# A hybrid decoder step: the projections of the 32 sample tokens as four partial sums in the four 32-column strips of the array

## The chip, the cores and the metric

The kernel runs on one core of one Trainium2 chip. The metric is the device time of one execution in microseconds (us). The kernel before takes 2430.94 us, the median of three runs (2429.08 to 2435.89).

## The reference, cut to what matters

One inference step of a two-layer decoder with model width 1024, for a prompt of 2048 tokens and for 8 decode sequences of 4 tokens each, the 32 "sample" tokens. Both pass through the same weights:

```python
def even_mixer(h, w_in, ...):            # layer 0: HGRN2 heads beside forgetting-attention heads
    proj = h @ w_in                      # 1024 -> 4100 columns
    ...
    out = jnp.concatenate([o_a, o_b], axis=-1) @ w_out
def odd_mixer(h, w_in, ...):             # layer 1: GLA
    proj = h @ w_in                      # 1024 -> 3088 columns
    ...
    return o @ w_out, s
```

All is float32. Each layer starts with an RMSNorm, ends with a residual add, and a last RMSNorm follows layer 1. What the change touches is a few of the matrix products above, and of them the rows of the 32 sample tokens alone: (32 x 1024) times (1024 x 256, 260 or 272).

## The kernel before, in words

**Numbers.** A float32 matrix product is made of three float16 products: activations and weights are each split into a high and a low half (`act` and `W`, both of class `Parts`, L95: a pair of views of one tile), and `mm3` (L451) adds high x high, high x low and low x high in PSUM. The fourth, low x low, isn't needed. The sum over 1024 rows takes 8 steps of 128, so a full product is 24 matmuls.

**Tokens.** The prompt is worked off in two halves of 1024 tokens. The 32 sample tokens ride with the first half, as columns 1024 to 1055 of `act`.

**Units.** The weights come in units of 256 columns (one of 260, one of 272). `half_unit` (L301) returns steps that fetch, measure, scale and split a unit, and `staged` (L1040) runs these steps for later units between the pieces of the present unit's product. There are two kinds of product. `proj_fm` (L457) is feature-major: the weights stand in the array and the tokens stream. `proj_tm` (L466) is token-major: 128 tokens stand in the array, 256 weight columns stream, two token tiles share a PSUM tile, and a function `evac` takes the result out.

**The sample tile in `proj_tm`.** With the first half come nine token tiles, eight of 128 tokens and one of 32. For units of 256 columns the tile of 32 goes to `few_rows` (L485). It first copies the sample tokens, once for all units of a stage, into a small tile `sam` that holds high and low halves side by side (L492, VectorE). Then 8 matmuls, one for each 128 rows of the sum, have the 64 columns (32 high, 32 low) standing and 512 columns streaming, which are 256 high and 256 low weight columns (`W.both`):

```python
nc.tensor.matmul(ps[: 2 * TS], self.sam[:, k].rearrange("p a t -> p (a t)"), W.both[:, :, k, :256], ...)
```

This gives all four products in four places of one PSUM tile `pS`. ScalarE copies one of them out (L498), VectorE adds two others to it (L500, two instructions), and low x low is left behind. The two wide units, `Bv0` (260 columns) and `Cv0` (272), take the ordinary way: 24 matmuls of `mm3` with 32 columns standing, evacuated from PSUM straight away.

**Which units are token-major.** In the first half of layer 0's input projection: `Ai0`, `Ai1` (`mk_v`, L793; their tiles are named `Av`), `Bk0`, `Bk1`, `Bv1` and the wide `Bv0` (`mk_bkv`, L870). In layer 0's output projection for the first half: `o00` to `o03` (`out_units`, L1610). In layer 1's input projection for the first half: the wide `Cv0` and `Cv1`, `Cv2`, `Cv3` (`mk_v`, L1666). In layer 1's output projection for the first half: `o10` to `o13`. These are 16 units of 256 columns and the two wide ones. For `Cv0` the last 16 columns are `r`, the input of the gate, which VectorE scales (L1685 to L1687), TensorE transposes (L1689, `prT`) and VectorE stores (L1690).

**PSUM.** The results of projections use the tag `pj`, with 3 buffers; `gr` has 2, `st` 1 and `o` 2.

**What sets the order.** Python generators issue the instructions. `mux` (L73) interleaves two generators by the costs that they yield: linear attention of one head (`lin_attn`, L512) runs beside the units of the next heads. After `few_rows`, `proj_tm` yields a cost of 1400 to it; other tiles yield 24 x 110 for each token tile. A scheduler then orders each engine's instructions by its own estimate of times, and each engine runs its list strictly in that order. So an instruction that waits holds back all that stand behind it on its engine.

**Work beside the sample tiles.** Within `lin_attn`, `levels` (L579) makes small matmuls (`gl`, L598) in strips of the array, and `decode` (L635) works on the states of the 8 sequences: `oS` (L676), four matmuls in four strips of 32 columns, then for every pair of sequences `stS` (L683, TensorE), a decay on GpSimd (L685) and an add on VectorE (L687). `stS` has one PSUM buffer, so each has to wait for the add of the one before it. In the attention over the paged cache there are two more places with four matmuls in four strips: the scores (L1416) and the forget biases (L1445).

## Time and profile before

| | |
|---|---|
| time of the profiled execution | 2431.39 us |
| its span, first to last instruction | 2429.7 us |
| around the span | 1.7 us |
| TensorE (PE) busy | 2316.8 us, 95% |
| VectorE (DVE) busy | 1463.1 us, 60% |
| ScalarE (ACT) busy | 1139.3 us, 47% |
| GpSimd (POOL) busy | 759.6 us, 31% |
| mean granted TensorE clock | 0.985 |

Times in the profile are microseconds from the start of the span, durations of single instructions are nanoseconds where it says so. PE is TensorE's matmuls, PEld its weight loads, which overlap the matmuls. L495 is line 495 of the kernel. A tile's name leaves out the buffer numbers: `pS_o` is the PSUM tile of `few_rows` in the output projections, whichever unit it is. In a row of the timeline stand the start, the time from the first start to the last end, the engine, the line, the operation, `out<-in`, the shape, and how many instructions of one kind were merged. A shape such as 128\*32 128x256 is a matmul with 128 rows and 32 columns standing in the array and 256 columns streaming. The end of a matmul is modelled and takes in its way through the array, so the times from start to start are what is to be read. Brackets at the end of a row give the time for which the engine was idle before it, and what ended that.

### The profile page before, as it was taken

The numbers are of one execution on the slowest core, as the hardware profiler recorded it, in microseconds if no ns is written. First come the engines' busy times: TensorE is split into PE (matmuls) and PEld (weight loads), VectorE is DVE, ScalarE is ACT, GpSimd is POOL, SyncE is SP. The second block draws the span as 40 slices with busy tenths as digits, with TensorE's granted clock in tenths as the row PEclk, the third lists the DMA queues.
The fourth block names the chain that finished last, engine by engine and source line by source line (L and its number), as shares of the span: only waits on it lengthen the run. The fifth ranks groups of instructions, "written<-read, shape, count | busy, mean of one in ns | idle before, by whom it ended". The sixth has DMA issues, their size and how long they took to land. (4 is left out here: it accounts for less than half of the span.)

```text
span 2429.7 us, 54346 instructions
## 1 busy us (share of the span) xinstructions
PE 2316.8 (95%) x21116; PEld 1637.8 (67%) x21116; DVE 1463.1 (60%) x3339; ACT 1139.3 (47%) x2513; POOL 759.6 (31%) x840
## 2 busy tenths in 40 slices
PE   7999999999999989999998999999999999998998
PEld 5667668855655875655445786777778766666887
DVE  7666657446765638667767353665675555557564
ACT  6434343343433126566667354545543645545243
POOL 3233323012213215234454221432443222322233
PEclk9999999999999999999999999999999999999999
DMA  6222235435431276776864631222246312114454
GB/s 183 73 80 80 67 111 166 142 107 146 144 115 59 85 227 204 227 250 205 274 209 141 191 107 44 63 75 76 67 141 192 117 37 70 44 58 152 142 195 153
DMA packets 296996, 316.97 MB, mean 130 GB/s; under 512 B 39729, under 2 KB 241010, under 8 KB 296738
## 3 DMA queue, kind: packets, MB, share of 16 engines
q1 hardware_dynamic: 295234, 308.98, 40.3%
q0 software_dynamic: 1504, 4.52, 0.5%
q8 instruction: 166, 2.72, 0.5%
q14 instruction: 92, 0.75, 0.1%
HBM read 242.31 MB, written 71.11 MB: 129 GB/s over the span
## 5 line engine op out<-in xcount | busy, mean ns | idle before, releaser
L453 PE MATMUL pt_o<-w_o,act 128*128 128x256 f16 x1024 | 282.8, 276 | 6.0 <-ACT w_o L335 5.1
L454 PE MATMUL pt_o<-w_o,act 128*128 128x256 f16 x1024 | 282.6, 276 | 1.1 <-POOL w_o L336 1.1
L455 PE MATMUL pt_o<-w_o,act 128*128 128x256 f16 x1024 | 282.6, 276 | 0.0
L453 PEld LDWEIGHTS <-act 128*128 128x128 f16 (+1 forms) x2320 | 228.7, 99 | 45.1 <-issue 14.3
L454 PEld LDWEIGHTS <-act 128*128 128x128 f16 (+1 forms) x2320 | 228.3, 98 | 33.1 <-issue 2.7
L455 PEld LDWEIGHTS <-act 128*128 128x128 f16 (+1 forms) x2320 | 228.4, 98 | 32.9 <-issue 4.3
L455 PE MATMUL pt_Cv<-w_Cv,act 128*128 128x256 f16 (+1 forms) x520 | 142.4, 275 | 0.0
L453 PE MATMUL pt_Cv<-w_Cv,act 128*128 128x256 f16 (+1 forms) x520 | 142.2, 275 | 0.0
L454 PE MATMUL pt_Cv<-w_Cv,act 128*128 128x256 f16 (+1 forms) x520 | 142.0, 275 | 0.0
L632 POOL TENSOR_TENSOR kA<-kA,fA 128x512 f32<-128x512 f32 (+1 forms) x56 | 80.8, 1442 | 195.7 <-PE gl_A L598 109.3
L1206 ACT ACTIVATE L<-L,nm,kc 128x512 f32<-128x512 f32 (+3 forms) x160 | 118.2, 741 | 35.5 <-DVE nm L1204 24.6
L632 POOL TENSOR_TENSOR kC<-kC,fC 128x512 f32<-128x512 f32 (+1 forms) x56 | 85.2, 1522 | 157.0 <-PE gl_C L598 76.4
L1214 POOL TENSOR_SCALAR L<-L,nm 128x512 f32<-128x512 f32 (+3 forms) x160 | 98.0, 626 | 79.3 <-DVE nm L1210 37.0
L1241 ACT ACTIVATE th<-pt 128x512 f16<-128x512 f32 (+3 forms) x159 | 80.4, 528 | 67.2 <-PE pt L1234 66.3
L1242 DVE TENSOR_TENSOR tl<-pt,th 128x512 f16<-128x512 f32 (+3 forms) x159 | 94.5, 608 | 25.9 <-ACT th L1241 25.3
L1234 PE MATMUL pt<-ident,L 128*128 128x128 f32 x544 | 91.0, 280 | 5.9 <-POOL L L1214 3.4
L1358 PEld LDWEIGHTS pkt<-ident,pgcache_fox_k 128*128 128x128 f32 x512 | 58.5, 143 | 46.7 <-issue 25.6
L1234 PEld LDWEIGHTS pt<-ident,L 128*128 128x128 f32 x544 | 67.2, 144 | 32.3 <-DVE tl L1242 8.4
L1358 PE MATMUL pkt<-ident,pgcache_fox_k 128*128 128x128 f32 x512 | 76.4, 282 | 11.4 <-DMA pgcache_fox_k<-in_cache_fox_k 7.8
L631 DVE TENSOR_TENSOR qC<-qC,fC 128x512 f32<-128x512 f32 (+1 forms) x56 | 53.5, 956 | 31.1 <-PE gl_C L598 30.2
L453 PE MATMUL pt_Bv<-w_Bv,act 128*128 128x256 f16 (+2 forms) x264 | 72.2, 273 | 0.0
L455 PE MATMUL pt_Bv<-w_Bv,act 128*128 128x256 f16 (+2 forms) x264 | 72.2, 273 | 0.0
(1088 smaller groups left out, 6887.8 us busy)
## 6 DMA issues: line engine op xcount, KB each, us to landing
pgcache_fox_k<-in_cache_fox_k SPq DMA_DIRECT2D x128, 256.0 KB, 4.1
pgcache_fox_v<-in_cache_fox_v SPq DMA_DIRECT2D x128, 256.0 KB, 4.0
yr<-yT SPq DMA_DIRECT2D x16, 1024.0 KB, 5.9
nx<-in_x_prompt SPq DMA_DIRECT2D x16, 512.0 KB, 4.8
wr_Aqf<-in_w_in_even SPq DMA_DIRECT2D x64, 128.0 KB, 2.8
wr_o<-in_w_out_even SPq DMA_DIRECT2D x32, 256.0 KB, 4.0
wr_Cv<-in_w_in_odd SPq DMA_DIRECT2D x32, 256.0 KB, 3.6
wr_Cqk<-in_w_in_odd SPq DMA_DIRECT2D x64, 128.0 KB, 2.6
```

What stands on the lines that cost most here:

```text
L453: nc.tensor.matmul(ps, lh[0], rh[0], start=first, stop=False)
L454: nc.tensor.matmul(ps, lh[0], rh[1], start=False, stop=False)
L455: return nc.tensor.matmul(ps, lh[1], rh[0], start=False, stop=last)
L631: nc.vector.tensor_tensor(xv[:, :, 1], xv[:, :, 1], t0.to_broadcast([P, nb, w]), ALU.mult)
L632: nc.gpsimd.tensor_tensor(kv[:, :, 0], kv[:, :, 0], t1.to_broadcast([P, nb, w]), ALU.mult)
L1206: self.last_exp = nc.scalar.activation(lt[:, :w], lt[:, :w], AF.Exp, bias=nm[:, 0:1], scale=ib, accum_out=nm[:, 2 + j : 3 + j])
L1214: nc.gpsimd.tensor_scalar(lt[:, :w], lt[:, :w], nm[:, 1:2], 2.0**14, ALU.mult, ALU.mult)
L1234: nc.tensor.transpose(pt[:, w : w + P], rows[b][s // 4][0][:, (s % 4) * P : (s % 4 + 1) * P], self.ident)
L1241: nc.scalar.activation(th[:, a:w], pt[:, a:w], AF.Copy),
L1242: nc.vector.tensor_tensor(tl[:, a:w], pt[:, a:w], th[:, a:w], ALU.subtract)))
L1358: nc.tensor.transpose(pk[:, j * P : (j + 1) * P], pgs[j][:, h * P : (h + 1) * P], self.ident)
```

## The change

`few_rows` no longer lets all four products come out of one wide matmul. It makes the three that are needed as matmuls of their own, 24 in all, each with 32 columns standing and the unit's width streaming. The 8 steps of the sum over 1024 rows are dealt out to four strips of 32 array columns: strip j takes steps j and j + 4 of each product, 6 matmuls that add up in PSUM partitions 32j to 32j + 31. Matmuls for the four strips are issued in turn. Then ScalarE copies strip 0's sum out, and VectorE adds those of the strips 1, 2 and 3, three adds in place of two. The wide units go the same way now, so `proj_tm` no longer has a path for a tile of 32 tokens, and the cost that it yields after `few_rows` is 700 in place of 1400. `Parts` no longer keeps the undivided tile.

```diff
@@ class Parts
-        self = super().__new__(cls, (both[:, 0], both[:, 1]))
-        self.both = both
-        return self
+        return super().__new__(cls, (both[:, 0], both[:, 1]))
@@ proj_tm
-            if n < P and width == 256:
-                evac(self.few_rows(pps, act, W, grp[0][0], nm), g, 1, n)
-                yield 1400
+            if n < P:
+                evac(self.few_rows(pps, act, W, grp[0][0], nm, width), g, 1, n)
+                yield 700
                 continue
@@ few_rows
-        ps = pps.tile([P, 2, 256], F32, tag="pj", name=f"pS_{nm}")
-        for k in range(KT):
-            nc.tensor.matmul(ps[: 2 * TS], self.sam[:, k].rearrange("p a t -> p (a t)"), W.both[:, :, k, :256],
-                             start=k == 0, stop=k == KT - 1)
-        t = self.few.tile([P, 512], F32, tag="c2", name=f"few_{nm}")[:TS, :256].unsqueeze(1)
-        nc.scalar.activation(t[:, 0], ps[:TS, 0], AF.Copy)
-        for r, c in ((0, 1), (TS, 0)):
-            nc.vector.tensor_tensor(t[:, 0], t[:, 0], ps[r : r + TS, c], ALU.add)
+        ps = pps.tile([P, width], F32, tag="pj", name=f"pS_{nm}")
+        for r in range(0, KT, 4):
+            for p, (x, y) in enumerate(((0, 0), (0, 1), (1, 0))):
+                for j in range(4):
+                    nc.tensor.matmul(ps[j * TS : (j + 1) * TS], self.sam[:, r + j, x], W[y][:, r + j, :width],
+                                     start=r + p == 0, stop=r > 0 and p == 2, tile_position=(0, j * TS))
+        t = self.few.tile([P, 512], F32, tag="c2", name=f"few_{nm}")[:TS, :width].unsqueeze(1)
+        nc.scalar.activation(t[:, 0], ps[:TS], AF.Copy)
+        for j in range(1, 4):
+            nc.vector.tensor_tensor(t[:, 0], t[:, 0], ps[j * TS : (j + 1) * TS], ALU.add)
         return t
```

In the order of the changed program, the 24 matmuls of a tile mostly stand together. In ten of the 18 tiles something stands between them: a transposition or a few small matmuls (`gl`, `stS`, `BkT`, `nt`), or some dozen matmuls of the next product. In `Cv1`, `Cv2` and `Cv3` these are `gl` and one `stS` pair after the first 10 of the 24 matmuls; before, they stood behind the whole tile and two more matmuls.

More of the change, by code (lines that the diff above doesn't have):

```diff
@@ L483, in proj_tm, with few_rows @@
             yield 24 * len(grp) * 110
-    def few_rows(self, pps, act, W, c0, nm):
+    def few_rows(self, pps, act, W, c0, nm, width):
         nc = self.nc
```

## The prediction

> **What bounds the kernel now.** I read the page first, then busy time by stage, then the timeline at the sample tiles.

> ```profile
> span 2429.7 us, 54346 instructions
> PE 2316.8 (95%) x21116; PEld 1637.8 (67%) x21116; DVE 1463.1 (60%) x3339; ACT 1139.3 (47%) x2513; POOL 759.6 (31%) x840
> PEclk9999999999999999999999999999999999999999
> ```

> ```profile
> 0.00:888.00 888.00, 854.65 (x8202) 602.67 (x8203) 537.74 (x1203) 337.63 (x763) 224.49 (x221) 1.00 0.37 113
> 888.00:1323.00 435.00, 399.31 (x2788) 233.86 (x2786) 297.76 (x931) 271.89 (x616) 196.11 (x311) 0.97 0.68 221
> 1475.00:2225.00 750.00, 729.98 (x7071) 523.30 (x7068) 443.19 (x818) 380.47 (x796) 237.12 (x207) 1.00 0.28 88
> 2225.00:2421.00 196.00, 192.06 (x1922) 165.35 (x1922) 109.41 (x212) 70.97 (x182) 59.48 (x64) 0.97 0.48 161
> ```

> TensorE is the bound: the first column after the length is its busy time, 96% of layer 0's projections (0 to 888 us), 97% of layer 1's (1475 to 2225) and 98% of the last products; its clock is nearly full. All sample tiles lie outside the attention stage (888 to 1323), the loosest. So time taken off TensorE's queue comes off the end, unless TensorE then arrives earlier at something that isn't ready. I therefore work out what a tile costs now, what it will cost, and at which places another engine eats the difference.

> **What a tile costs now.** One of the 16 narrow tiles, with the full-array matmuls around it:

> ```profile
> 391.27 0.27 PE L454 MATMUL pt_Bk<-w_Bk,act 128*128 128x256 f16 x1
> 391.38 0.27 PE L455 MATMUL pt_Bk<-w_Bk,act 128*128 128x256 f16 x1
> 391.58 1.92 PE L495 MATMUL pS_Bk<-w_Bk,sam_Av 128*64 128x512 f16 x8
> 393.43 0.28 PE L453 MATMUL pt_Bv<-w_Bv,act 128*128 128x260 f16 x1
> ```

> ```profile
> L495 PE MATMUL pS_o<-w_o,sam_o x64: 379/379/635, 1357.2 to 2336.9; 128*64 128x512 f16 x64
> L495 PE MATMUL pS_Cv<-w_Cv,sam_Cv x24: 379/379/404, 1540.3 to 1722.6; 128*64 128x512 f16 x24
> L495 PE MATMUL pS_Av<-w_Ai,sam_Av x16: 379/379/404, 51.9 to 217.8; 128*64 128x512 f16 x16
> L495 PE MATMUL pS_Bk<-w_Bk,sam_Av x16: 378/379/404, 391.6 to 453.1; 128*64 128x512 f16 x16
> L495 PE MATMUL pS_Bv<-w_Bv,sam_Av x8: 379/379/403, 484.3 to 485.9; 128*64 128x512 f16 x8
> ```

> From the last full-array matmul (391.38) to the next one (393.43) pass 2.05 us. Between full-array matmuls the step is 0.11 us (391.27 to 391.38); going over to 64 standing columns it is 0.20 (391.38 to 391.58). 64 + 24 + 16 + 16 + 8 = 128 matmuls, by 8 a tile: 16 tiles. A wide tile:

> ```profile
> 426.27 0.27 PE L455 MATMUL pt_Bv<-w_Bv,act 128*128 128x260 f16 x1
> 426.47 0.28 PE L453 MATMUL pt_Bv<-w_Bv,act 128*32 128x260 f16 x1
> 429.03 0.27 PE L455 MATMUL pt_Bv<-w_Bv,act 128*32 128x260 f16 x1
> 429.24 0.28 PE L453 MATMUL pt_Bk<-w_Bk,act 128*128 128x256 f16 x1
> ```

> 24 matmuls one after another, (429.03 - 426.47) / 23 = 0.111 us each, with the same 0.20 to go over and 0.21 to come back: 2.97 us. This also shows that a load of 32 columns per matmul fits behind 260 streamed columns of float16, in one strip.

> **What it will cost.** No float16 matmuls stand side by side in this trace, but float32 ones do:

> ```profile
> 1116.86 1.06 PE L1416 MATMUL sc<-kts,qz 128*32 128x512 f32 x8
> 1117.74 1.06 PE L1445 MATMUL sc<-suf,sel 128*32 128x128 f32 x32
> 1118.73 0.39 PE L453 MATMUL s<-h_k,h_q 128*128 128x512 f16 x1
> L1445 PEld LDWEIGHTS sc<-suf,sel x32: 109/110/111, 1117.3 to 1118.4; 128*32 128x32 f32 x32
> 2323.93 0.60 PE L563 MATMUL py_C<-ident,on_C 128*128 128x128 f32 x4
> ```

> L1445 runs 32 records, eight waves over the four strips. One alone would stream for about 0.11 us: the four full-array records of the last row take (0.60 - 0.28) / 3 = 0.107 from start to start, with 0.28 us the length of one, about that of the fp16 rows above. In a line 32 would need 3.5 us. They need 0.99 (1117.74 to 1118.73) with the way back to the full array: seven waves of 0.11 and 0.22 after the last one's start. The loads, one for each record and 110 ns long, don't show. A float16 matmul of 256 columns streams as long as such a record (0.11 us, rows above), so I take a **wave of 0.11 us**. Six waves: 0.20 + 5 x 0.11 + 0.22 = 0.97 us against 2.05, a gain of 1.08. The wave is bounded from below by the stream of one matmul, 0.11, and from above by four in a line, 0.44. I take 1.05, since the row's first wave comes from strips already and mine comes from the full array.

> [...]

> **The places.** Four full-mode interruptions cost a second way out and in, about 0.2 us each: in the changed order such work stands within `Av0`, `Av1`, `Bk0` and `o00`, where before it stood outside or the modes were alike. In `o10` two switches go, as `gl`, itself in strips, now follows directly. Net -0.6 us.

> `Bv0` gains 2.97 - 0.97 = 2.0. `Cv0` was cut up by other work:

> ```profile
> 1463.89:1469.99 6.10, 6.10 (x40) 3.12 (x38) 1.53 (x8) 1.07 (x4) 0.00 (x0) 1.00 0.00 0
> 1465.42 0.23 DVE L1687 SCALAR_TENSOR_TENSOR rt<-pt_Cv,kc,rh 128x16 f32<-128x16 f32 x1
> 1466.15 0.31 PE L1689 MATMUL prT<-ident,rt 128*80 128x128 f32 x1
> ```

> Of the 6.1 us about 2.0 are 13 matmuls of the next product (0.15 each), so 4.1 are the tile, with its many switches, and small transpositions. Now it takes some 1.2 with one split. But in the new order the transposition of the last full tile's `r` stands before it, and its input comes only at 1465.65, 1.8 us after that tile's last matmul (1463.89); and the tile now needs VectorE's copies into `sam`. I take 0.5 us of gain, between 0 and 3.

> `Cv1`, `Cv2`, `Cv3` are where another engine is late:

> ```profile
> 1540.35 1.91 PE L495 MATMUL pS_Cv<-w_Cv,sam_Cv 128*64 128x512 f16 x8
> 1542.19 0.32 PE L453 MATMUL pf_C01q<-act,w_Cqk 128*128 128x352 f16 x1
> 1542.60 0.71 PE L598 MATMUL gl_C<-qC,kC 128*24 128x16 f32 x64
> 1544.34 0.50 PE L683 MATMUL stS_C<-hl_C,kpad_C 96*128 96x256 f32 x2 [1.04 <-DVE s_C L687]
> ```

> ```profile
> 1536.73 1.82 DVE L660 TENSOR_TENSOR kpad_C<-hl_C,rowmask 96x512 fp32r<-96x512 f32 x2
> ...
> 1542.30 1.27 DVE L704 TENSOR_TENSOR vp_C<-vC,vp_C 128x256 fp32r<-128x256 f32 x1
> 1543.60 0.69 DVE L687 TENSOR_TENSOR s_C<-s_C,stS_C 128x512 f32<-128x512 f32 x1
> ```

> `stS` waits for VectorE's add, and VectorE is busy without a gap from 1536.7 up to it, with nothing of the sample tile ahead. So `stS` stays at 1544.3 however fast the tile is. In the new order only 10 of the 24 matmuls stand before it. The other 14 (3.5 waves and the way in and out, some 0.7 us) come behind it, and so do the two matmuls of the next product that stood before it (0.3): TensorE is 1.0 us later after `stS` than now. The last waits of the same chain can give that back, as it doesn't move either:

> ```profile
> PE py_C00S L563 <- ACT scT L606: 1.1, 1, 1.1
> ```

> I take a loss of 0.5 us for each of the three, between a gain of 1.05 and a loss of 1.1.

> **The evacuation.**

> ```profile
> L500 DVE TENSOR_TENSOR few_o<-few_o,pS_o x16: 397/410/414, 1362.2 to 2342.7; 32x256 f32<-32x256 f32 x16
> PE pt_Av L453 <- ACT act L448: 1.2, 1, 1.2
> ```

> One more add of 0.41 us for each narrow tile and a copy with three adds for the wide ones: some 9 us of VectorE, of which 40% is free. It holds a `pj` buffer 0.4 us longer, while two others let TensorE run on for two products; I cost it at nothing, and without that cover it would be 0.41 x 16 = 6.6 us. `Bv1` comes just before the second half's normalization, where TensorE already waits 1.2 us for ScalarE: I take 0.5 off there, between 0 and 1.05.

> **The sum.** 13 narrow tiles x 1.05 = 13.65, `Bv0` 2.0, `Cv0` 0.5, `Cv1` to `Cv3` -1.5, splits -0.6, `Bv1` -0.5: 13.5 us. From the profiled execution's 2431.4 (0.45 over the median of the three runs) that gives **2418 us**. With every tile's gain kept it is 21 us, 2410; with all the bounds on the bad side, 6.6 us of evacuation among them, some 4 us are left, 2427.

> **The rivals.**
> *Half-speed waves.* The four float16 strips get their weights or their columns only half as fast as the float32 ones, a wave of 0.22 us. For it speaks that a float32 wave of 512 columns takes 0.44 us (1116.86 to 1117.74, two waves), twice the time per column, so the float32 rows never asked for four strips at one column per 0.42 ns; against it that a float32 column is twice as many bytes. A tile then takes 1.63 us: the gain is 0.4 x 13 = 5.2, `Bv0` 1.3, `Cv0` 0, `Cv1` to `Cv3` -0.9 each (3.5 waves longer by 0.11 behind `stS`), splits and `Bv1` -1.1: 2.7 us, **2429 us**. [...]
> *Strips in a line* (slower). If float16 strips do not overlap at all, 24 matmuls of 0.111 and 0.41 for the switches are 3.0 us, 1.0 more than now: 13 x 1.0, three times 1.7 at `Cv1` to `Cv3` (the 0.5 and 14 x 0.11 - 3.5 x 0.11 behind `stS`), and the 1.1 of splits and `Bv1`, a loss of 19 us: **2450 us**. The sum changes sign at a wave of about 0.25 us. L1445 speaks against it.
> *Given back by the order.* The scheduler moved instructions of VectorE and ScalarE in the attention stage too, where no line changed; TensorE idles there for 435 - 399 = 36 us, and a quarter more of that, 9 us, would leave **2427 us**.

> **How the numbers follow.** Forecast 0.78, half-speed waves 0.09, in a line 0.05, given back 0.08. The forecast's own range is 2410 to 2427; to hold the time 8 times in 10 with half the chance of the first rival, I go to 2429. About 0.3% (7.3 us) is what a measurement of this kernel can tell from no change. Of the forecast 0.72 lie below 2423.6 and 0.06 above it; with most of the two middle rivals "same" has 0.21. Slower: the line, and 0.02 of an order gone worse, 0.07.

> **What would show it.** In the changed profile a tile's 24 records (128*32 128x256) from its last full-array neighbour to the next: 1.0 us is the forecast, 1.6 the first rival, 3.0 the second. `stS` at `Cv1` to `Cv3` should wait 2 us or more for L687. VectorE's add should be 0.41 us, and TensorE's matmuls after a tile should not wait for a `pj` buffer. Wrong it would be if the wave is over 0.2 us, or if TensorE's idle time in the attention stage or in the last products grows by several us.

## The result and the profile after

The changed kernel takes 2426.8 us (median of 20 runs, 2421.08 to 2431.52), the kernel before 2431.13 (20 runs): a ratio of 0.9982, 95% interval 0.9975 to 0.9989. It is faster by 4.3 us, where 13.5 were forecast. The profiled execution has a span of 2422.9 us, 2424.6 with the 1.7 around it, 2 us below the median. In what follows `Av00` is the prediction's `Av0`, `Cv01` its `Cv1`, and so on: the first digit is the half.

Two lines from the head of the page after, then busy time by stage (the same stretches as before; columns: PE, PEld, DVE, ACT, POOL, granted clock, DMA):

```profile
span 2422.9 us, 54885 instructions
PE 2300.0 (95%) x21372; PEld 1631.5 (67%) x21372; DVE 1478.9 (61%) x3361; ACT 1140.2 (47%) x2515; POOL 749.4 (31%) x840
```

```profile
0.00:888.00 888.00, 851.22 (x8279) 600.62 (x8280) 541.13 (x1211) 337.75 (x764) 222.69 (x221) 0.99 0.37 113
888.00:1323.00 435.00, 396.88 (x2792) 232.96 (x2791) 301.83 (x936) 278.86 (x627) 203.16 (x316) 0.97 0.68 223
1475.00:2225.00 750.00, 723.83 (x7074) 519.73 (x7073) 448.64 (x828) 377.77 (x794) 237.33 (x208) 0.99 0.29 87
2225.00:2421.00 196.00, 186.57 (x1984) 163.08 (x1982) 112.77 (x214) 70.83 (x181) 55.38 (x65) 0.98 0.49 164
```

TensorE has 16.8 us less to do (2316.8 to 2300.0), but its span shrank by only 6.8: the work went, the time stayed as idle time. In the four rows TensorE's free time grew by 3.4, 2.4, 6.2 and 5.5 us (888 - 851.22 against 888 - 854.65, and so on; roughly, since the stages begin up to 7 us earlier now, so that the last row takes in more of the kernel's end). The clock column fell from 1.00 to 0.99 in both stages of projections, which looks like nothing; but the clock records of both traces have 1.00 and 0.50 alone, so a mean of 0.99 over 750 us means 15 us at half clock (2 x 0.01 x 750; the records have 15.9 in the third row).

The tile itself is what was forecast. A narrow one with its neighbours in the timeline after, and the third add:

```profile
453.65 0.27 PE L453 MATMUL pt_Bk<-w_Bk,act 128*128 128x256 f16 x1
453.86 0.84 PE L495 MATMUL pS_Bk<-w_Bk,sam_Av 128*32 128x256 f16 x24
454.62 0.49 PE L247 MATMUL spr_o<-ident,kc 128*128 128x128 f32 x2
```

```profile
L500 DVE TENSOR_TENSOR few_o<-few_o,pS_o x24: 411/416/423, 1356.3 to 2339.4; 32x256 f32<-32x256 f32 x24
L495 PEld LDWEIGHTS <-sam_o x192: 92/97/152, 1349.7 to 2328.9; 128*32 128x32 f16 x192
```

From neighbour to neighbour pass 0.97 us (453.65 to 454.62), to the hundredth the working of the prediction; the way in is 0.21 (453.65 to 453.86). The 24 loads of 97 ns, 2.3 us in a line, don't show; nor do those of one strip in the prediction's wide tile, at 0.111 us a matmul with a load each. So both rivals about waves are out, with their 1.63 and 3.0 us.

Where the time stayed is seen at `Cv01`, TensorE first, then VectorE, then the windows of the stretch:

```profile
1531.69 0.50 PE L495 MATMUL pS_Cv<-w_Cv,sam_Cv 128*32 128x256 f16 x10
1532.72 0.70 PE L598 MATMUL gl_C<-qC,kC 128*24 128x16 f32 x64 [0.53 <-DVE rst_C00S L384]
1535.69 0.50 PE L683 MATMUL stS_C<-hl_C,kpad_C 96*128 96x256 f32 x2 [2.26 <-DVE s_C L687]
1536.12 0.61 PE L495 MATMUL pS_Cv<-w_Cv,sam_Cv 128*32 128x256 f16 x14
...
1538.69 0.50 PE L452 MATMUL pf_C01q<-act,w_Cqk 128*128 128x352 f16 x1
1538.99 0.50 PE L453 MATMUL pf_C01q<-act,w_Cqk 128*128 128x352 f16 x1
...
1540.71 0.31 PE L452 MATMUL pf_C01q<-act,w_Cqk 128*128 128x352 f16 x1
1540.86 0.31 PE L453 MATMUL pf_C01q<-act,w_Cqk 128*128 128x352 f16 x1
```

```profile
1533.64 1.27 DVE L704 TENSOR_TENSOR vp_C<-vC,vp_C 128x256 fp32r<-128x256 f32 x1
1534.94 0.69 DVE L687 TENSOR_TENSOR s_C<-s_C,stS_C 128x512 f32<-128x512 f32 x1
```

```profile
1533.00:1535.00 2.00, 0.42 (x51) 0.33 (x35) 1.97 (x3) 0.00 (x0) 2.00 (x3) 1.00 0.04 8
1536.40:1538.00 1.60, 1.60 (x19) 0.77 (x8) 1.52 (x3) 1.23 (x3) 1.29 (x2) 0.58 0.47 164
1538.00:1539.80 1.80, 1.80 (x8) 0.88 (x6) 1.76 (x4) 1.41 (x3) 1.80 (x2) 0.50 0.08 27
1541.00:1544.00 3.00, 3.00 (x81) 2.08 (x79) 2.18 (x5) 1.71 (x5) 0.74 (x1) 1.00 0.24 50
```

`stS` waits 2.26 us for the add L687 in place of 1.04, as forecast ("2 us or more"). What was not forecast stands behind it: the same matmul of 352 columns comes every 0.30 us (1538.69 to 1538.99) and later every 0.15 (1540.71 to 1540.86), and the granted clock is 0.50 in between. Behind the idle stretch (1533.4 to 1535.7) TensorE's clock is at 0.50 for 3.4 us (1536.6 to 1540.0 in the clock's records), and at 0.30 us a matmul in place of 0.15 these 3.4 us do 1.7 us less work than at full clock. `Cv02` and `Cv03` look the same.

The first tile, `Av00`, before and after:

```profile
51.94 1.91 PE L495 MATMUL pS_Av<-w_Ai,sam_Av 128*64 128x512 f16 x8 [1.56 <-DVE sam_Av L492]
54.49 0.32 PE L453 MATMUL pf_Ag<-act,w_Ag 128*128 128x352 f16 x1 [0.22 <-ACT w_Ag L335]
55.73 0.32 PE L455 MATMUL pf_Ag<-act,w_Ag 128*128 128x352 f16 x1 [0.76 <-POOL w_Ag L336]
```

```profile
52.51 0.62 PE L495 MATMUL pS_Av<-w_Ai,sam_Av 128*32 128x256 f16 x16
54.66 0.32 PE L451 MATMUL pf_Ag<-act,w_Ag 128*128 128x352 f16 x1 [1.53 <-ACT w_Ag L333]
56.25 0.45 PE L451 MATMUL pf_Ag<-act,w_Ag 128*128 128x352 f16 x1 [1.11 <-DVE pow_Aqf L265]
```

```profile
55.00:56.00 1.00, 0.14 (x1) 0.00 (x0) 1.00 (x4) 0.36 (x1) 1.00 (x2) 0.63 0.02 4
56.00:62.00 6.00, 5.75 (x20) 2.89 (x20) 5.62 (x19) 2.06 (x7) 3.80 (x10) 0.50 0.41 117
```

The next unit's weights `w_Ag` are still being split by ScalarE. The old tile covered that; now TensorE waits for it, and then runs 6 us at half clock. And behind `Bk00` stands a wait that is 0.19 us in the profile of before:

```profile
400.08 0.49 PE L754 MATMUL o_A<-v,scT 128*128 128x128 f32 x2 [1.42 <-ACT scT L606]
```

### The profile page after: what moved, and what is told of

The parts are those of the page before. It is cut to its first block, busy times and chain, and to the rows that moved or that the text cites. A ratio compares the mean times of both kernels' runs of the same rounds, so it can differ in the third digit from the quotient of the medians.

```text
span 2422.9 us, 54885 instructions
## 1 busy us (share of the span) xinstructions
PE 2300.0 (95%) x21372; PEld 1631.5 (67%) x21372; DVE 1478.9 (61%) x3361; ACT 1140.2 (47%) x2515; POOL 749.4 (31%) x840
## 5 line engine op out<-in xcount | busy, mean ns | idle before, releaser
L453 PE MATMUL pt_o<-w_o,act 128*128 128x256 f16 x1024 | 282.8, 276 | 0.0
L451 PEld LDWEIGHTS <-act 128*128 128x128 f16 x2304 | 227.0, 99 | 44.4 <-issue 11.6
L452 PEld LDWEIGHTS <-act 128*128 128x128 f16 x2304 | 226.8, 98 | 34.9 <-issue 4.9
L453 PEld LDWEIGHTS <-act 128*128 128x128 f16 x2304 | 226.7, 98 | 33.0 <-issue 4.3
L451 PE MATMUL pt_Cv<-w_Cv,act 128*128 128x256 f16 (+1 forms) x512 | 140.1, 275 | 1.5 <-ACT act L446 0.9
L453 PE MATMUL pt_Cv<-w_Cv,act 128*128 128x256 f16 (+1 forms) x512 | 140.2, 275 | 0.0
L452 PE MATMUL pt_Cv<-w_Cv,act 128*128 128x256 f16 (+1 forms) x512 | 139.8, 275 | 0.0
L1241 ACT ACTIVATE th<-pt 128x512 f16<-128x512 f32 (+3 forms) x159 | 81.2, 528 | 71.6 <-PE pt L1234 70.5
L451 PE MATMUL pt_Av<-w_Ai,act 128*128 128x256 f16 x256 | 70.5, 276 | 1.9 <-ACT act L446 1.9
L452 PE MATMUL pt_Av<-w_Ai,act 128*128 128x256 f16 x256 | 70.4, 275 | 0.8 <-POOL w_Ai L334 0.8
```

What stands on the lines that cost most here:

```text
L451: nc.tensor.matmul(ps, lh[0], rh[0], start=first, stop=False)
L452: nc.tensor.matmul(ps, lh[0], rh[1], start=False, stop=False)
L453: return nc.tensor.matmul(ps, lh[1], rh[0], start=False, stop=last)
L1241: nc.scalar.activation(th[:, a:w], pt[:, a:w], AF.Copy),
```

## The experiments

The theory tested: the strips bring about 1 us each, but at `Av00` and `Cv01` to `Cv03` a shorter tile only makes TensorE wait longer for another engine, and a wait of this length costs half the clock behind it. Rivals: the forecast's own terms for these places without the clock (A); the gain is lost elsewhere, through the new order or the evacuation (B).

All runs in one table. The last column is the time at half clock, mean over all runs of the kernel: 2 x (1 - granted clock) x span.

| run | tiles in strips | ratio to before, 95% | us at half clock |
|---|---|---|---|
| before | none | 1 | 68.0 |
| changed kernel | 18 | 0.9982 (0.9975 to 0.9989) | 81.5 |
| e1_but_cv | 15 | 0.9970 (0.9959 to 0.9982) | 77.9 |
| e2_but_av_cv | 14 | 0.9951 (0.9935 to 0.9968) | 70.2 |
| e12, the same again | 14 | 0.9958 (0.9941 to 0.9974) | 68.3 |
| e3_only_av_cv | 4 | 0.9990 (0.9978 to 1.0001) | 72.9 |
| e7_cv123 | 3 | 1.0030 (1.0017 to 1.0043) | 73.1 |
| e5_late8 | 8 | 0.9984 (0.9969 to 0.9999) | 69.6 |
| e6_one_tile | 1 | 0.9994 (0.9977 to 1.0011) | 70.5 |
| e4_filled | 18 | 0.9986 (0.9972 to 0.9999) | 67.6 |
| e9_add_first | 18 | 0.9967 (0.9954 to 0.9980) | 78.3 |
| e10_before_add_first | none | 0.9998 (0.9986 to 1.0010) | 70.1 |
| e11_add_first_but_av | 17 | 0.9972 (0.9959 to 0.9986) | 73.2 |

e8 is the kernel before, profiled once more; that one execution took 2428.89 us.

### Four places taken out, and put in alone

In e1, e2, e3, e5, e6, e7 and e12 the old `few_rows` stands beside the new one as `few_old`, and a list of names decides (e1's is shown):

```diff
+            if n < P and nm in ("Cv01", "Cv02", "Cv03"):
+                evac(self.few_old(pps, act, W, grp[0][0], nm), g, 1, n)
+                yield 1400
+                continue
             if n < P:
                 evac(self.few_rows(pps, act, W, grp[0][0], nm, width), g, 1, n)
```

> Tiles Cv01, Cv02 and Cv03 keep the form of before (8 matmuls of 64 columns, one add less); all others in strips. Theory (a shorter tile only lengthens the wait of stS for VectorE, and the longer idle stretch brings a half-clock stretch of 3.4 us behind it, about 1.7 us lost at a place): the three places cost 1.4 to 2.3 us each in the changed kernel, so without them the time falls by about 5 us against the changed kernel, to 0.9961 of before (2421.5 us); the waits at stS are about 1 us again and no half-clock stretch follows there. Rival A (the forecast's own terms: 0.5 us each, no clock): 1.5 us less than the changed kernel, 0.9976 (2425). Rival B (the lost gain comes from the new order or the evacuation elsewhere): within 0.5 us of the changed kernel, 0.998.

> Also Av00 in the form of before: the four places that the theory names are out, 14 tiles in strips. Theory: Av00 gains nothing in strips (TensorE waits for ScalarE's and VectorE's split of the next unit's weights) and loses 1 to 1.8 us by the half clock behind it: about 1.3 us below the run without Cv01 to Cv03 alone, 0.9955 of before (2420 us). Rival A (Av00 gains 1.05 us as in the forecast): 1.05 us above that run. Rival B: no difference.

> The kernel with the four places in the form of before once more, since its interval was wide: 0.9951 again within 0.0015.

> Only Cv01, Cv02 and Cv03 in strips; the order of the attention stage is that of before. Theory: each loses 0.5 us by the matmuls moved behind stS and about 1.25 by the half-clock stretch behind the longer wait: 5 us slower, 1.0021 of before, and some 10 us more at half clock in each run. Rival A (the forecast): 1.5 us slower, 1.0006, and no more half clock. Rival B (a later wait of the same chain, py for ScalarE, gives the clock's loss back): 1.5 us slower or less although 10 us more run at half clock.

> The reverse: only Av00, Cv01, Cv02 and Cv03 in strips, everything else (the wide tiles too) as before. Theory: the losses alone, 3 x 1.8 + 1.3 = 6.7 us slower than before, 1.0028 (2438 us), with half-clock stretches behind all four. Rival A (the forecast's terms): 1.5 lost, 1.05 gained, 1.0002. Rival B (the loss comes from the order in other stages or from the wide tiles): within 1 us of before.

Without the four places the kernel is at 0.9951 and 0.9958, 11 us below before, and the time at half clock is back at that of before. So four of 18 tiles eat 6.6 us (0.9982 less about 0.9955, by 2431). Rival B is out for them. e7 shows it from the other side: three tiles in strips and nothing else make the kernel 7.3 us slower (4.1 to 10.5), more than the theory's 5 and far more than rival A's 1.5. But its time at half clock is only 5.1 us above that of before (73.1 against 68.0), where some 10 were expected. At the rate worked out below that is 2.3 of the 7.3 us; what the other 5 are is open. e1 lies between theory and A, and doesn't tell them apart.

e3 went against the theory: 6.7 us slower was expected, it is 2.4 us faster (0.2 slower to 5.3 faster). Part of this is the order of the attention stage (below), which made that stage 3.6 us shorter in e3's profile and is unchanged in e7; the rest stays open. Contributions of single places don't add up in this kernel.

### The wait or the clock?

e3's trace holds a comparison that nobody arranged. The three places run the same instructions with the same waits (rows of `stS`), but the stretch behind the third runs at full clock (windows of 3 us, from 1.5 us after each `stS`):

```profile
1540.96 0.51 PE L706 MATMUL stS_C<-hl_C,kpad_C 96*128 96x256 f32 x2 [2.26 <-DVE s_C L710]
1725.15 0.50 PE L706 MATMUL stS_C<-hl_C,kpad_C 96*128 96x256 f32 x2 [2.26 <-DVE s_C L710]
```

```profile
1542.50:1545.50 3.00, 3.00 (x13) 1.49 (x11) 2.94 (x6) 2.19 (x4) 2.58 (x3) 0.52 0.22 78
1634.60:1637.60 3.00, 3.00 (x13) 1.55 (x11) 2.94 (x6) 2.19 (x4) 2.60 (x3) 0.53 0.24 82
1726.70:1729.70 3.00, 3.00 (x22) 1.96 (x20) 2.94 (x6) 2.18 (x4) 2.59 (x3) 1.00 0.22 78
```

13 matmuls in 3 us against 22. From the transposition `ktS` to the first product of the head's gate unit the three passes take 41.57, 41.57 and 39.89 us. In the traces of the changed kernel, e3 and e7 there are nine passes with strips: eight with 3.4 us at half clock, 41.33 to 41.57, and this one without. With the old tile there are 21 (before, e1, e2, e5, e6, e8, e12): seventeen without half clock take 39.05 to 40.75, mean 39.72; the other four, e6's three and e5's last, have their half clock behind `py` and take 41.34 to 44.01. So where both run at full clock, a strip tile at these places costs 0.2 us by the longer wait and the matmuls behind `stS` (39.89 less 39.72, one pass against a spread of 1.7), less than the 0.5 of the forecast; where the half clock comes, it adds 1.6 (mean of the eight, 41.51, less 39.89). Over all passes as they fell, strips cost 1.1 (41.33 less 40.21). These are fewer draws than they look: the three passes of an execution lie 92.1 us apart, 27 times the 3.41 us of a half-clock stretch, and so mostly meet it alike.

Two experiments tried to take the clock's part away alone. The first fills the wait with work (`wide` is the tile's PSUM buffer with room for 512 columns):

```diff
+        if nm in ("Av00", "Cv01", "Cv02", "Cv03"):
+            for k in range(KT):
+                nc.tensor.matmul(wide[:TS], self.sam[:, k, 0], W.both[:, :, k, :256], start=True, stop=True)
```

> The changed kernel, with eight extra matmuls of 512 columns (1.8 us; their sums are overwritten by nothing that is read) ahead of the strips of Av00, Cv01, Cv02 and Cv03 alone: more work for TensorE, at places where it waits anyway. It tells the two halves of the theory apart. If the half clock behind a long wait is what costs, the time falls although work is added: the waits at stS go from 2.3 to about 0.8 us, no half-clock stretch follows, 1.2 us saved at each of the three and 1.5 at Av00, less 0.2 to 0.3 each for strips that move behind stS: 4 us below the changed kernel, 0.9966 of before (2422.7 us). If the clock does not matter and only the wait does, nothing is saved and 0.2 to 0.3 us is lost at each place: 1 us above the changed kernel, 0.9986.

It doesn't decide. The time, 0.9986, is what was expected if the clock doesn't matter. The half clock behind `stS` and at `Av00` went, and the time at half clock fell from 81.5 to 67.6 us, but `stS` still waits 1.46 us and the extra matmuls moved the order: at `Cv01` to `Cv03` `py` now stands ahead of `zC`, waits 1.4 to 1.5 us in two pieces in place of 0.8, and in two of three places brings a half-clock stretch of its own. At `Av00` the transposition `spr_Aqf` stands behind the fill.

The second leaves TensorE's order as it is and exchanges two instructions of VectorE, so that `stS` waits less:

```diff
+                    add = nc.vector.tensor_tensor(sb, sb, st, ALU.add)
+                    if half == 0 and x == 0:
+                        self.first_add = add
...
+                        if hf == 0:
+                            e.enter_context(self.tc.issue_after(self.first_add.ins))
+                        vp.append(vpart(1))
```

> The changed kernel with two instructions of VectorE exchanged at Cv01 to Cv03: the add of the first state block (L687, for which stS waits) now stands ahead of the second piece of vp (L704, 1.27 us); TensorE's order is the same, and all tiles are in strips. Theory: the wait of stS falls from 2.26 to 1.0 us, and with it the half-clock stretch behind it goes: 3 x (1.27 + 1.67 x 0.9) = 8.3 us less than the changed kernel, 0.9948 of before. Rival (VectorE itself is the bound of the place and hands the wait to the next product of the chain): the waits at stS fall, those at py grow as much, within 1.5 us of the changed kernel.

> The same exchange of two instructions in the kernel before: the wait of 1.04 us at stS goes, there is no half-clock stretch to lose: 3 x 1.04 = 3.1 us less than before, 0.9987. What the exchange brings the changed kernel beyond this is the longer wait and the clock that the strips brought. Rival as for the run above: no difference, 1.000.

> The exchange, and Av00 in the form of before, all other tiles in strips: the version that the runs so far point to. The three places keep what a shorter tile brings, Av00 loses nothing: 2 us less than the run with the exchange alone (Av00 in strips took 28.7 us against 26.6 from the tile to the first product of the unit behind it), 0.994 of before, about 2416 us.

TensorE's waits in sum (us, times, longest), each kernel by itself: before, e10, after, e9.

```profile
PE stS_C L683 <- DVE s_C L687: 6.2, 5, 2.1
PE zC L1705 <- ACT qC L1719: 0.6, 2, 0.3
```

```profile
PE zC L1711 <- ACT qC L1725: 5.1, 7, 2.9
PE stS_C L683 <- DVE s_C L687: 2.1, 1, 2.1
```

```profile
PE stS_C L683 <- DVE s_C L687: 9.9, 5, 2.3
PE zC L1705 <- ACT qC L1719: 1.1, 1, 1.1
```

```profile
PE stS_C L683 <- DVE s_C L687: 5.3, 4, 2.1
PE zC L1711 <- ACT qC L1725: 4.3, 7, 1.1
```

The waits went from `stS` to `zC` almost whole: 6.8 us became 7.2 in the kernel before, 11.0 became 9.6 in the changed one. That is the rival's case; it had named `py` as the heir, and it is `zC`, which waits for `q` by way of ScalarE. The times agree: e10 brings nothing; e9 is some 3.6 us below the changed kernel (0.9967 against 0.9982, the intervals overlap), where the theory wanted 8.3. In two of e9's three passes a half-clock stretch now follows `zC` and `py`, whose waits of about 1 us each fall close together. e11, with the exchange and 17 tiles, is no faster than e2 without it and 14. So these places look bound by the chain through VectorE and ScalarE, and TensorE time saved there hardly reaches the end.

### One tile, and the stage that nobody touched

> Only tile Bk01 in strips. The instructions of the attention stage come in the changed order (that of the runs with Av00 kept, with Av00 filled), where no line is changed. Theory: in the profiles of all changed kernels so far that stage is 4.5 to 7 us shorter than in the one profile of before, so its order is worth about 4.5 us and one tile 1.05: 5.5 us, 0.9977 of before. Rival: that stage's length in before's profile was chance (half-clock stretches that fall otherwise in other runs): 1 us, 0.9996.

> The kernel before, profiled once more: the attention stage (first score matmul of the prompt to the third key block) took 156.2 us in its first profile and 149.2 to 151.6 in those of the changed kernels. If the order sets it, 156 again (within 1); if the half-clock stretches do, it is shorter by 1.7 for each that does not return.

The attention stage, from its first score matmul to the third key block, before and after:

```profile
888.30:1044.50 156.20, 136.73 (x978) 86.65 (x975) 101.09 (x304) 86.34 (x194) 59.88 (x103) 0.95 0.73 240
```

```profile
889.70:1039.00 149.30, 134.55 (x976) 86.22 (x977) 99.73 (x303) 86.32 (x194) 60.95 (x103) 0.97 0.74 246
```

TensorE's instructions come in three orders at the head of this stage. With that of before the stretch takes 155.9 to 156.2 us in five profiles (before, e5, e7, e8, e10); with that of the changed kernel 149.2 to 149.8 in three (after, e1, e9); with that of e2, e3, e4, e6, e11 and e12 151.4 to 155.0. In after, e1, e3, e4 and e9 TensorE waits 0.99 us for VectorE's `Bv` just ahead of the stretch; with it the changed order is 5 to 6 us shorter than that of before. So the order is the cause, not chance (before and e7, e1 and e9 have 13.7 to 17.1 us at half clock in the stretch alike), and it gave the changed kernel 5 to 6 us in the profiles that belong to no term of the forecast. e6, with the third order (153.1 in its profile) and one tile, should gain 4; its interval runs from 5.6 us faster to 2.7 slower, so the time can't confirm it.

> Only the eight output tiles (o000 to o003, o100 to o103) in strips; the order of the attention stage is that of before. No other engine is waited for behind these tiles. If a tile is worth 1.05 us where nothing is waited for, eight bring 8.4 less 0.2 for a split: 8.2 us, 0.9966 of before (2424 us), at an unchanged clock. If the tile's gain itself is smaller than the trace suggests (the rival: VectorE's extra add or the two switches take part of it), 4 us or less, above 0.9984.

Eight tiles behind which no wait was expected bring 3.9 us (0.2 to 7.5), not 8.2. In the traces the four tiles of layer 0 shorten their stretch by 3.1 to 3.4 us (changed kernel, e1, e2, e5, e12) and the four of the last products theirs by 2.5 to 3.4. That is 0.6 to 0.85 a tile, below 1.05: part of each is lost to small waits and switches that I haven't separated.

## Why the prediction missed

**The step that failed** is the sentence "time taken off TensorE's queue comes off the end, unless TensorE then arrives earlier at something that isn't ready". The exception was asked for at `Cv0` to `Cv3` and `Bv1` alone, and there the idle time of TensorE was taken for free. At `Av0`, `Bk0` and `Bv0` full gains were counted, and the evacuation was put at nothing.

**The tile: right.** 0.97 us against 0.97, the add 0.416 against 0.41. As forecast, matmuls hardly wait for a `pj` buffer that an add frees; there is one such wait in the profile after:

```profile
PE pt_Cv L451 <- DVE few_o L500: 0.6, 1, 0.6
```

**`Cv1` to `Cv3`, "a loss of 0.5 us for each of the three": too small.** Its mechanism was right in every part (the add doesn't move, `stS` waits longer, 14 matmuls fall behind it), and at full clock it costs 0.2 us in the one pass that shows it. What was left out is the half clock. In the traces a place costs 1.1 us over all passes, 1.8 against the passes of the old tile without half clock (41.51 less 39.72): 3.4 to 5.4 for the three, and 7.3 in e7's time, where the sum had 1.5.

**`Av0`, counted as one of "13 narrow tiles x 1.05": wrong.** `w_Ag` isn't ready there. From the tile's first matmul to the first product of `A00f`, the unit behind `Ag`, pass 26.6 us in all nine profiles with the old tile (and no fill), and 28.7, 28.7, 28.3 and 28.0 with strips: a loss of 1.4 to 2.1 in place of a gain of 1.05. All four have the half clock, so its share here is only argued. `Bk0` is the same without the clock: its 1.08 went into the 1.42 of `o_A`. That wait is 1.2 to 2.9 us in all seven profiles with `Bk00` in strips and at most 0.2 in the other seven.

**`Bv0`, "2.0", and the evacuation, "I cost it at nothing": wrong together.** The wide tile's result used to be taken from PSUM by VectorE straight away; now ScalarE's copy comes first. Before, then after:

```profile
429.35 0.21 DVE L884 SCALAR_TENSOR_TENSOR lf<-pt_Bv,kc,bfox 32x4 f32<-32x4 f32 x1 [1.43 <-PE pt_Bv L455]
437.44 0.60 PE L914 MATMUL BkT<-ident,Bk 128*128 128x128 f32 x4
```

```profile
433.54 0.72 ACT L332 ACTIVATE wr_Aqf<-wr_Aqf,kc 128x512 f32<-128x512 f32 x1 [2.91 <-DMA wr_Aqf<-in_w_in_even]
434.17 0.36 ACT L498 ACTIVATE few_Bv<-pS_Bv 32x260 f32<-32x260 f32 x1
438.82 0.75 DVE L889 TENSOR_SCALAR Bk<-pt_Bk,kc 128x512 f32<-128x512 f32 x1
439.62 0.65 PE L914 MATMUL BkT<-ident,Bk 128*128 128x128 f32 x4 [0.64 <-DVE Bk L889]
```

The tile is done at about 430.6, but the copy stands behind an instruction of ScalarE that waits for the DMA of `wr_Aqf` until 433.54. The three adds and VectorE's other work come behind the copy, `Bk` behind them, and `BkT` on TensorE waits for `Bk`: 0.6 to 2.0 us in all seven profiles with `Bv00` in strips, not at all in the other seven. To that extent rival B holds outside the four places; no run changes this alone.

**Layer 0's input projections together.** From `Av00`'s first matmul to the first score of the attention pass 833.1 to 836.3 us in the five profiles with old tiles throughout (before, e5, e7, e8, e10; 0 to 6.8 us of it at half clock), 838.0 to 843.1 in the three with strips throughout (changed kernel, e1, e9; 17.1 to 20.5) and 834.6 to 840.7 in the three with strips but for `Av00` (e2, e11, e12; 3.4 to 17.1). The terms of the forecast for this stretch add up to a gain of 6.1 us (5 x 1.05 + 2.0 - 0.5 - 0.6). In the profiles nothing of it is left.

**The clock as a term.** It stood in the prediction as "nearly full". Over 225 runs of all kernels, compared within each kernel, a microsecond at half clock costs 0.45 us (standard error 0.02). The changed kernel has 13.5 us more of it than before, worth 6.0 us. With the 4.3 measured that is 10.3 us at equal clock. Of the 6.6 us between the changed kernel and e2 and e12 the same rate puts 5 to 6 down to the clock (81.5 against 70.2 and 68.3), of e7's 7.3 only 2.3.

**The order.** "Given back by the order" was a rival with a loss of 9 us; the order did act, in the other direction, and covered up part of the miss. That is luck.

In sum, the two profiled executions by stretches (how much later the same TensorE instructions start, median around each mark; negative is shorter, times are those of before):

| stretch, us | forecast | after less before |
|---|---|---|
| 51 to 885, layer 0's input projections | -6.1 | +0.1 |
| 885 to 1340, attention | 0 | -6.9 |
| 1340 to 1455, layer 0's output projection | -4.0 | -1.3 |
| 1455 to 1530, with `Cv00` | -0.5 | -0.8 |
| 1530 to 1740, with `Cv01` to `Cv03` | +1.5 | +6.1 |
| 1740 to 2225 | 0 | -1.4 |
| 2225 to 2420, last products | -4.4 | -3.1 |

That is 7.3 us where 13.5 were forecast and the medians of the runs differ by 4.3. A row holds the draw of the half clock as well: e8, the same program as before, differs from it by 3.2 us in the first. So the direction of each miss is seen, but what each is worth over many executions isn't. That, and why e3 and e7 lie 9.7 us apart, would need the half-clock stretches of many executions; a profile shows those of one.

The version to keep is that of e2 and e12: strips for 14 tiles, the old form for `Av00` and `Cv01` to `Cv03`, 11 us below before and 6.6 below the changed kernel. With `Bv00` in the old form too it was not run.

## What to carry to other kernels

Before counting a gain on the busiest engine, ask at each place what it waits for next: a shorter piece of work ahead of a late input was worth nothing here (`Av00` lost 1.4 to 2.1 us, where 1.05 were to be gained). Ask the same of the result: a copy put on another engine's list starts only when that list reaches it (the one of `few_Bv` 3.6 us after its tile was done, 430.6 to 434.17). On TensorE a shorter piece can be worth less than nothing, as at `Cv01`: behind `stS`'s wait of 2.26 us in place of 1.04 came 3.4 us at half clock. Where most places gain and a few wait, change the places, not the function.

## What the runs showed of the hardware

The two profiles of the same kernel, before and e8, have the phases 0.16 and 1.06 us. If the phase is drawn anew in each execution, as they suggest, the same kernel takes other times: e6's runs cover 16 us, and within them time and mean clock go together (correlation -0.94).
